# Normalising the input tiles in four pinned steps at the pace of the chunks, in a three-mixer decoder layer

## The chip, the cores and the metric

The kernel runs on one core of a Trainium2 chip. The metric is the device time of one launch in microseconds (us), the median of several runs. TensorE (PE in the profile) multiplies matrices; VectorE (DVE), ScalarE (ACT) and GpSimd (POOL) work on tiles; SyncE (SP) issues the DMAs of this kernel. Each engine works through its own list of instructions strictly in order.

## What the reference computes, cut to what matters

One layer of a decoder is applied to a prompt of 2048 tokens of 1024 features and to eight single sample tokens. All three mixers read the same normalised input h:

```python
h = rmsnorm(x, g_norm)            # x * rsqrt(mean(x*x) + EPS) * g
proj = h @ w_in_l                 # one projection, columns split among A, B, C
ya = swa_prompt(q, k, v, ...)     # A: softmax attention, window 128, 8 heads
yb, v_rows = chunk_mlp(ub, vb, ...)   # B: gated MLP in chunks of 128
oc, S_fin = gla(qc, kc, vc, ...)  # C: gated linear attention
y = concat([ya * silu(ga), yb * silu(gb), yc * silu(gc)])
x = x + y @ w_out_l               # and a last rmsnorm
```

## The kernel before, in words

**Tiles and chunks.** x comes in 16 tiles of 128 tokens (`NTILE`). Two tiles make a chunk of 256 tokens (`CT`), so there are 8 chunks. For each chunk the kernel builds `hT[c]`, the normalised input transposed to features on partitions, as two f16 parts, high and low; all eight stay in SBUF. A projection is three matmuls for each block of 128 features (`PASSES`: high*high, high*low, low*high).

**How one tile is made.** `x_load(t)` (L241) fetches 128x1024 floats into one of four buffers. `norm_split` does five things: ACT squares the tile and sums each row (L245, "square"); DVE scales the sum (L247) and takes its reciprocal root in nine instructions on one column (L125, L126, L127 and three times L131 and L135; together with L247 this is "root"); ACT writes the tile times that factor as f16 (L249, "high"); DVE computes what f16 lost (L250, "low"). `h_tile` then issues two DMA transposes on SP (L259), one for each part. `hs_prep` does the same for the eight sample tokens, and sends them through DRAM.

**Phase A, the first 310 us or so.** For each chunk PE computes two value units (evicted by ACT L471 and DVE L472), one key unit (ACT L450 and L451, DVE L452 and L453, each twice), four query units (ACT L491, DVE L492, each twice) and two gate units (ACT L501 takes the tanh, DVE L502 multiplies). The two gates of chunk c are called here its first and second gate. Chunks 0 and 1 come first with both gates behind them; from chunk 2 on the gates follow their chunk. The projection of x reads `hT[c]`, so chunk c can't begin before its tiles are transposed.

Beside it runs the softmax of 32 half-tiles, four to a chunk: scores on PE (L521), scale, bias and row maximum on DVE (L525, four to a half-tile), three small steps on DVE (L535, L537, L539), then on ACT the sink's exponent (L542), which also opens the four exponents (L553), a cast to f16 (L563), on POOL the part that f16 lost (L564), two transposes on SP (L578), and on PE the product with V (L593), evicted on DVE (L598, L600). L566, L572 and L573 on DVE are the row sums' reciprocal.

**What sets the order.** `at(t, f)` emits step f when the planned time of the matmuls emitted so far, counted from their columns, passes t. A chunk's plan is `TQ` = 15.68 for its value, key and query units and 10.24 for its two gates, so `TC` = 25.92; this clock of the plan runs faster than the chip. A scheduler then places the emitted instructions on each engine by its own estimate; only those that are wrapped in `keep_in_program_order` keep their order among one another. In the kernel before, tile t is emitted at `HT0 + HTD * (t - 4)`, 22, 33, 44 and so on, one tile for 11 planned us; that is faster than the 12.96 that half a chunk takes, and the tiles' instructions aren't pinned.

Phases B and C and the output projection follow. The weights of B (`LOADP["B0"]`, `LOADP["B1"]`) are loaded during phase A, behind the tiles.

Of the kernel before, what the change touches and what calls it, by code (L numbers as in the profile page):

```python
# [12 lines left out]
BF16 = mybir.dt.bfloat16  # L13
I32 = mybir.dt.int32
U32 = mybir.dt.uint32
AF = mybir.ActivationFunctionType
ALU = mybir.AluOpType
# [6 lines left out]
DM = 1024  # L24
DMIX = 1536
EPS = 1e-6
# [17 lines left out]
def hybrid_step_kernel(ctx: ExitStack, tc: tile.TileContext, I, O):  # L44
    nc = tc.nc
    V, S, G, PE, SP = nc.vector, nc.scalar, nc.gpsimd, nc.tensor, nc.sync
# [17 lines left out]
    HT0, HTD, HTL = 22, 11, 18  # L64
    WB = {"pha": 1, "phb": 1, "yy": 6}

    def nm(s):
        cnt[0] += 1
        return f"{s}_{cnt[0]}"
# [13 lines left out]
    def hbuf(shape, dt):  # L83
        return hp_.tile(shape, dt, tag="hT", name=nm("hb"))

    def slot(shape, dt):
        return sl_.tile(shape, dt, tag="slot", name=nm("sl"))
# [31 lines left out]
    def chain(p, n):  # L119
        t = sm.tile([p, 8 * n], F32, tag=f"ch{n}", name=nm("ch"), bufs=CHB[n])  # L120
        return [t[:, i * n:(i + 1) * n] for i in range(8)]

    def rsqrt(ch, n):
        v, vh, y, b = ch[0], ch[1], ch[2], ch[3]
        V.tensor_scalar(out=vh, in0=v, scalar1=-0.5, scalar2=None, op0=ALU.mult)  # L125
        V.tensor_scalar(out=y.bitcast(I32), in0=v.bitcast(I32), scalar1=1, scalar2=None, op0=ALU.logical_shift_right)  # L126
        V.tensor_scalar(out=y.bitcast(I32), in0=y.bitcast(I32), scalar1=-1.0, scalar2=float(0x5F3759DF),  # L127
                        op0=ALU.mult, op1=ALU.add)
        for _ in range(3):
            if n == 1:  # L130
                V.scalar_tensor_tensor(out=b, in0=y, scalar=vh, in1=y, op0=ALU.mult, op1=ALU.mult)  # L131
            else:
                V.tensor_tensor(out=b, in0=y, in1=y, op=ALU.mult)
                V.tensor_tensor(out=b, in0=b, in1=vh, op=ALU.mult)
            V.scalar_tensor_tensor(out=y, in0=b, scalar=1.5, in1=y, op0=ALU.add, op1=ALU.mult)  # L135
        return y
# [11 lines left out]
    LOADP = {}  # L148
# [67 lines left out]
    def stage_slot(n):  # L216
        def f():
            return [(slot([128, 8, n], F32), 0, 8)]
        return f

    def dst_slot(n):
        return lambda: slot([128, 2, 8, n], F16)
# [4 lines left out]
    hT = {}  # L227
    xst = {}

    def h_alloc(c):  # L230
        hT[c] = hbuf([128, 2, 8, CT], F16)

    def x_bufs(j):
        if not xst:
            xst[0], xst[1] = slot([128, 4096], F32), slot([128, 4096], F32)
        b = xst[j // 2][:, (j % 2) * 2048:(j % 2 + 1) * 2048]
        return b[:, 0:DM], b[:, DM:2 * DM].bitcast(F16).rearrange("p (a b) -> p a b", a=2)

    def x_load(t):
        xt, _ = x_bufs(t % 4)  # L240
        SP.dma_start(out=xt, in_=xp[t * 128:(t + 1) * 128, :])  # L241

    def norm_split(xt, xh, p):
        ch = chain(p, 1)
        S.activation(out=xh[:, 0, :].bitcast(BF16), in_=xt, func=AF.Square, accum_out=ch[4])  # L245
        q = 2.0 ** -20
        V.tensor_scalar(out=ch[0], in0=ch[4], scalar1=q / DM, scalar2=q * EPS, op0=ALU.mult, op1=ALU.add)  # L247
        rs = rsqrt(ch, 1)
        S.activation(out=xh[:, 0, :], in_=xt, func=AF.Copy, scale=rs)  # L249
        V.scalar_tensor_tensor(out=xh[:, 1, :], in0=xt, scalar=rs, in1=xh[:, 0, :], op0=ALU.mult, op1=ALU.subtract)  # L250

    def h_tile(t):
        c, j = divmod(t, 2)
        if j == 0:
            h_alloc(c)
        xt, xh = x_bufs(t % 4)
        norm_split(xt, xh, 128)
        for hl in range(2):
            SP.dma_start_transpose(out=hT[c][:, hl, :, j * 128:(j + 1) * 128], in_=xh[:, hl, :])  # L259

    def hs_prep():
        xt, xh = x_bufs(0)
        xt, xh = xt[:NB], xh[:NB]
        SP.dma_start(out=xt, in_=xs)
        norm_split(xt, xh, NB)
        for hl in range(2):
            SP.dma_start(out=hs_d[hl * 8:(hl + 1) * 8, :], in_=xh[:, hl, :])
        h16 = sm.tile([128, 8, 16], F16, tag="h16", name="h16", bufs=1)
        SP.dma_start_transpose(out=h16, in_=hs_d)
        G.memset(hs, 0.0)  # L270
        G.tensor_copy(out=hs[:, :, 0:16], in_=h16)
        V.tensor_reduce(out=selg, in_=ident.rearrange("p (g c) -> p c g", c=8), axis=AX.X, op=ALU.add)
# [4 lines left out]
    def at(t, *fs):  # L277
        for f in fs:
            cnt[0] += 1
            bisect.insort(EV, (t, cnt[0], f))  # L280
# [1037 lines left out]
    if True:  # L1318
# [21 lines left out]
        for f in prA0[1:]:  # L1340
# [3 lines left out]
        prB = [prep_slice(f"B{i}", 3 + i, [(OFF[n], 512)], stage_slot(512), dst_slot(512))  # L1344
               for i, n in enumerate(("vb", "gb", "ub"))]
# [16 lines left out]
        TQ, TG, TC = 15.68, 20.48, 25.92  # L1362
# [15 lines left out]
        at(7.0, lc_bm(0))  # L1378
        at(9.0, lc_bm(1))
        for t in range(4, NTILE):  # L1380
            at(HT0 + HTD * (t - 4) - HTL, lambda t=t: x_load(t))
            at(HT0 + HTD * (t - 4), lambda t=t: h_tile(t))
        at(HT0 + HTD * 12, hs_prep)
        at(11.0, prA2[1])
        at(14.0, prA2[2], prA2[3])
        at(18.0, prA2[4], consts_A)
        tb = HT0 + HTD * 12 + 4
        for f, d in zip(LOADP["B0"] + prB[0][1:], (0, 3, 6, 9, 12, 20, 21.5, 24)):
            at(tb + d, f)
        tb += 24  # L1390
        for i, f in enumerate(LOADP["B1"]):
            at(tb + 3 * i, f)
        tb = TB - 12
        for f, d in zip(prB[1][1:], (0, 8, 9.5, 11)):
            at(tb + d, f)
# [45 lines left out]
        for c in range(NCH):  # L1441
# [29 lines left out]
            if c in (4, 5, 6):  # L1471
                i = c - 4
# [71 lines left out]
```

## Time and profile before

| what | value |
|---|---|
| median of 3 runs | 1185.88 us (1183.29 to 1186.48) |
| the profiled execution: its time, its span | 1185.16 us, 1183.4 us |
| PE busy | 1127.1 us, 95% of the span, 7623 matmuls |
| DVE busy | 681.8 us, 58% |
| ACT busy | 477.1 us, 40% |
| POOL busy | 72.6 us, 6%, nearly all of it the 32 instructions of L564 |
| mean granted clock of PE | 0.988 of full speed |

The profiled execution took 1.76 us more than its span, and lies 0.7 us under the median. The busy share of PE is a mean over stages: for most of the span it has next to no idle time, and the places where it has some are in phase A.

### The profile page before, as it was taken

To read this page: it belongs to the slowest core of one execution; us is meant where nothing else is said; L and a number is where in the kernel's file an instruction comes from. 1 tells how busy PE (TensorE), PEld (TensorE's weight loads), DVE (VectorE), ACT (ScalarE), POOL (GpSimd) and SP (SyncE) were. 2 spreads that over 40 slices of the span, in tenths; PEclk is the share of its full clock that TensorE was granted. 3 is DMA by queue.
4 is the path that set the end of the run, shared out by engine and by line. 5 is a ranking of instruction groups with operands and counts; after the bars stand their busy time and mean duration, and the time that the engine had idled before them with its cause. 6 is when DMAs were issued, how large, how long until landed. Compare 5 with 4: busy or idle time off the path is not lost.

```text
span 1183.4 us, 19624 instructions
## 1 busy us (share of the span) xinstructions
PE 1127.1 (95%) x7623; PEld 661.8 (56%) x7623; DVE 681.8 (58%) x2236; ACT 477.1 (40%) x960; POOL 72.6 (6%) x49
## 2 busy tenths in 40 slices
PE   4897899997999999999999999999999999999997
PEld 3756577775645544444466567656665543444443
DVE  5896866658586355675383356744635653544442
ACT  7776665567572111553265411312312132322220
POOL 0021222222210000000000000000000000000000
PEclk9998999999899999999999999999999999999999
DMA  9579964445454012000055422220124345766641
GB/s 275 162 135 192 194 153 90 70 85 127 104 145 117 18 59 96 1 19 18 19 187 168 173 73 47 89 81 19 59 50 143 121 114 150 223 156 159 165 126 54
DMA packets 202055, 131.17 MB, mean 111 GB/s; under 512 B 160225, under 2 KB 174818, under 8 KB 201962
## 3 DMA queue, kind: packets, MB, share of 16 engines
q1 hardware_dynamic: 201962, 129.92, 42.5%
q8 instruction: 59, 0.97, 0.4%
q14 instruction: 34, 0.28, 0.1%
HBM read 67.21 MB, written 25.33 MB: 78 GB/s over the span
## 4 chain that ended last, share of the span: by engine, by line
PE 58%; DMA 5%; DVE 4%; ACT 3%; issue 1%; SPq 1%; DVEq 0%; ACTq 0%
PE pp L308 31%; PE pp L1027 13%; PE pp L297 6%; DMA hb<-sl 2%; PE mx L886 1%; PE mx L690 1%; PE mx L868 1%; ACT sl L996 1%; DMA sq_d<-yy 1%; PE mx L892 1%; PE mx L900 1%; DMA sl<-in_w_out_dram 1%; DMA sl<-y_d 1%; SPq L1008 1%; DVE sl L1016 1%
## 5 line engine op out<-in xcount | busy, mean ns | idle before, releaser
L308 PE MATMUL pp<-sl,hb 128*128 128x512 f16 x2304 | 516.3, 380 | 1.3 <-DVE qk L492 1.3
L308 PEld LDWEIGHTS <-hb 128*128 128x128 f16 x2688 | 248.4, 99 | 265.7 <-issue 8.0
L1027 PE MATMUL pp<-hb,hb 128*128 128x512 f16 x1152 | 251.1, 379 | 3.1 <-DMA hb<-sl 3.1
L1027 PEld LDWEIGHTS <-hb 128*128 128x128 f16 x1152 | 111.7, 98 | 140.9 <-DMA hb<-sl 6.2
L297 PE MATMUL pp<-hb,sl 128*128 128x256 f16 x1536 | 180.2, 276 | 10.6 <-DVE yy L502 10.5
L297 PEld LDWEIGHTS <-sl 128*128 128x128 f16 x1536 | 150.3, 99 | 34.2 <-issue 12.9
L564 POOL TENSOR_TENSOR phb<-Lp,pha 128x1024 f16<-128x1024 f32 (+1 forms) x32 | 66.5, 2077 | 283.3 <-ACT pha L563 267.1
L1030 DVE SCALAR_TENSOR_TENSOR sl<-pp,finv,sl 128x512 f32<-128x512 f32 x32 | 23.9, 747 | 86.1 <-PE pp L1027 86.0
L501 ACT ACTIVATE yy<-pp,scal 128x512 f32<-128x512 f32 x48 | 32.5, 680 | 84.9 <-PE pp L308 62.0
L1013 ACT ACTIVATE sl<-sl 128x1024 f32<-128x1024 f32 (+1 forms) x16 | 16.9, 1056 | 117.1 <-DVE sl L1030 115.0
L553 ACT ACTIVATE Lp<-Lp,sm 128x256 f32<-128x256 f32 (+1 forms) x128 | 62.3, 487 | 0.2
L525 DVE CUSTOM_DVE_ANT_0 Lp<-mx,BM,scal 128x256 f32<-128x256 f32 (+1 forms) x128 | 54.6, 471 | 2.0 <-PE mx L521 1.4
L502 DVE SCALAR_TENSOR_TENSOR yy<-yy,pp 128x512 f32<-128x512 f32 x48 | 32.7, 682 | 38.1 <-ACT yy L501 38.0
L492 DVE SCALAR_TENSOR_TENSOR qk<-pp,qk 64x256 f16<-64x256 f32 x64 | 26.9, 422 | 38.8 <-ACT qk L491 37.8
L642 ACT ACTIVATE kk<-pp,invs 128x512 f32<-128x512 f32 x16 | 10.9, 683 | 83.3 <-PE pp L308 83.3
L997 DVE SCALAR_TENSOR_TENSOR sl<-sl,ch 128x1536 f16<-128x1536 f32 (+1 forms) x17 | 30.9, 1816 | 20.4 <-ACT sl L996 20.3
L996 ACT ACTIVATE sl<-sl,ch 128x1536 f16<-128x1536 f32 (+1 forms) x17 | 26.8, 1576 | 32.1 <-DVE ch L145 32.1
L521 PE MATMUL mx<-kk,qk 128*128 128x256 f16 (+1 forms) x256 | 33.3, 271 | 3.6 <-DVE sm L525 3.6
L205 DVE SCALAR_TENSOR_TENSOR sl<-sl,gs,sl 128x512 f16<-128x512 f32 x48 | 35.1, 791 | 1.7 <-ACT sl L204 1.7
L308 PE MATMUL pp<-s,hb 128*128 128x144 f16 x384 | 29.7, 236 | 6.2 <-DMA hb<-sl 4.0
L656 DVE BATCH_NORM_STATS2 sm<-kk 128x6 f32<-128x512 f32 x16 | 11.0, 689 | 41.5 <-ACT kk L642 41.5
L563 ACT CAST pha<-Lp 128x1024 f16<-128x1024 f32 (+1 forms) x32 | 32.4, 1011 | 5.0 <-DMA pt<-pha 4.6
(316 smaller groups left out, 1227.2 us busy)
## 6 DMA issues: line engine op xcount, KB each, us to landing
sl<-in_x_prompt_dram SPq DMA_DIRECT2D x32, 512.0 KB
sl<-in_w_in_dram SPq DMA_DIRECT2D x24, 512.0 KB
sl<-in_w_out_dram SPq DMA_DIRECT2D x6, 2048.0 KB
sl<-y_d SPq DMA_DIRECT2D x16, 768.0 KB
y_d<-yy SPq DMA_DIRECT2D x32, 256.0 KB
out_dram<-sl SPq DMA_DIRECT2D x15, 512.0 KB
hb<-in_w_in_dram SPq DMA_DIRECT2D x8, 512.0 KB
y_d<-Lp SPq DMA_DIRECT2D x8, 512.0 KB
```

The source lines that it names most:

```text
L205: V.scalar_tensor_tensor(out=lo, in0=src, scalar=gk, in1=hi, op0=ALU.mult, op1=ALU.subtract)
L297: PE.matmul(ps[:m, :CT], w[:, wl, k, c0:c0 + m], h[:, hl, k, :], start=(n == 0), stop=(n == 23))
L308: PE.matmul(ps[:, :n_], h[:, hl, k, j * 128:(j + 1) * 128], w[:, wl, k, c0:c0 + n_], start=(n == 0), stop=(n == 23))
L501: S.activation(out=g, in_=ps, func=AF.Tanh, scale=hg)
L502: V.scalar_tensor_tensor(out=g, in0=g, scalar=1.0, in1=ps, op0=ALU.add, op1=ALU.mult)
L521: PE.matmul(pv[:, hh, :], Qt[c][:, h // 2, h % 2, j * 128:(j + 1) * 128], Kt[c][:, 2 * hb + hl, ko:ko + W], start=(hl == 0), stop=(hl == 1))
L525: V.tensor_tensor_reduce(out=L[:, i, :], in0=pv[:, hh, :], in1=BM["t"][:, 4 * hb + i, 256 - W:256], scale=cS, scalar=-3e38, op0=ALU.add, o ...
L553: S.activation(out=L[:, i, :], in_=L[:, i, :], func=AF.Exp, bias=nb[:, i:i + 1], accum_out=den[:, i:i + 1])
L563: S.copy(P[0], L)
L564: G.tensor_tensor(out=P[1], in0=L, in1=P[0], op=ALU.subtract)
L996: S.activation(out=d["h"][:, 0, :], in_=d["y"], func=AF.Copy, scale=s)
L1027: PE.matmul(ps, d["yT"][:, hl, k, :], wo[k // 2][:, wl, k % 2, cs], start=(n == 0), stop=(n == 35))
```

## The change

`norm_split` and `h_tile` stay for the first four tiles and the samples. For tiles 4 to 15 a new `h_steps(t)` returns the same work as four functions, and the loop emits them at four planned times: square at `th`, root 5 later, high 9 later, low with both transposes 11 later. `th` follows the chunk: 22, 29.84, 43.76, 55.76, 69.7, 81.7, 95.6, 107.6, 121.5, 133.5, 147.4 and 159.4 for tiles 4 to 15, so two tiles for each 25.92 planned us. The first instruction of each step is pinned. `x_load` stays 18 ahead of its tile. The samples' preparation moves from 154 to 173.4, the loads and preparation of B0 from 158 to 167.4 with shorter distances, B1's loads from 182 to 180.4 and closer together.

```diff
+    def h_steps(t):
+        st = {}
+        def square():
+            if t % 2 == 0:
+                h_alloc(t // 2)
+            st["x"], st["h"] = x_bufs(t % 4)
+            st["ch"] = chain(128, 1)
+            tc.keep_in_program_order(S.activation(out=st["h"][:, 0, :].bitcast(BF16), in_=st["x"], func=AF.Square,
+                                                  accum_out=st["ch"][4]))
+        def root():
+            ch = st["ch"]
+            q = 2.0 ** -20
+            tc.keep_in_program_order(V.tensor_scalar(out=ch[0], in0=ch[4], scalar1=q / DM, scalar2=q * EPS,
+                                                     op0=ALU.mult, op1=ALU.add))
+            st["rs"] = rsqrt(ch, 1)
+        def high():
+            tc.keep_in_program_order(S.activation(out=st["h"][:, 0, :], in_=st["x"], func=AF.Copy, scale=st["rs"]))
+        def low():
+            tc.keep_in_program_order(V.scalar_tensor_tensor(out=st["h"][:, 1, :], in0=st["x"], scalar=st["rs"],
+                                                            in1=st["h"][:, 0, :], op0=ALU.mult, op1=ALU.subtract))
+            c, j = divmod(t, 2)
+            for hl in range(2):
+                SP.dma_start_transpose(out=hT[c][:, hl, :, j * 128:(j + 1) * 128], in_=st["h"][:, hl, :])
+        return square, root, high, low
...
-            at(HT0 + HTD * (t - 4) - HTL, lambda t=t: x_load(t))
-            at(HT0 + HTD * (t - 4), lambda t=t: h_tile(t))
-        at(HT0 + HTD * 12, hs_prep)
+            th = max(HT0, 2 * TQ + TG + TC * (t // 2 - 2) - 34 + 12 * (t % 2))
+            at(th - HTL, lambda t=t: x_load(t))
+            for f, d in zip(h_steps(t), (0, 5, 9, 11)):
+                at(th + d, f)
+        at(th + 14, hs_prep)
...
-        tb = HT0 + HTD * 12 + 4
-        for f, d in zip(LOADP["B0"] + prB[0][1:], (0, 3, 6, 9, 12, 20, 21.5, 24)):
+        tb = th + 8
+        for f, d in zip(LOADP["B0"] + prB[0][1:], (0, 2, 4, 6, 10, 18, 19.5, 21)):
...
-        tb += 24
+        tb += 13
         for i, f in enumerate(LOADP["B1"]):
-            at(tb + 3 * i, f)
+            at(tb + 2 * i, f)
```

In the changed kernel the new function pushes every later line 30 down: L502 becomes L532, L525 becomes L555, L566 becomes L596, L472 becomes L502, and so on. Its four steps are L260 (square), L266 (root, with L125 to L135), L271 (high) and L274 (low).

Three places show what the change does to an order. The first is DVE at the second gate of chunk 1 in the kernel before, where the low steps (L250) of three tiles stand among softmax and key evictions:

```order
L566 TENSOR_TENSOR sm_1357<-sm_1235,sm_1236 128x4
L250 SCALAR_TENSOR_TENSOR sl_107<-sl_107,ch_2052 128x1024
L572 RECIPROCAL sm_1359<-sm_1357 128x4
L535 TENSOR_TENSOR sm_1416<-sm_1326,sinkb 128x4
L598 TENSOR_TENSOR yy_1216<-mx_1379,rc_980 128x256
L573 TENSOR_SCALAR rc_1181<-sm_1359,scal 128x4
L452 SCALAR_TENSOR_TENSOR kk_1365<-pp_1296,kk_1365 64x256
L453 SCALAR_TENSOR_TENSOR kk_1365<-pp_1296,kk_1365 64x256
L600 TENSOR_TENSOR yy_1216<-yy_1216,yy_1034 128x256
L537 TENSOR_SCALAR sm_1418<-sm_1416 128x4
L250 SCALAR_TENSOR_TENSOR sl_107<-sl_107,ch_2300 128x1024
```

By the end of chunk 2's second gate all sixteen tiles have been made in the kernel before; from chunk 3 on DVE's order holds no tile. The second place is DVE at the first gate of chunk 4 in the changed kernel, where the root of an even tile (here tile 12) now stands between the gate and the four scores of the next half-tile (L555); in the kernel before L525 follows L502 here without anything between:

```order
L532 SCALAR_TENSOR_TENSOR yy_2857<-yy_2857,pp_2760 128x512
L266 TENSOR_SCALAR ch_2792<-ch_2792 128x1
L125 TENSOR_SCALAR ch_2792<-ch_2792 128x1
L126 TENSOR_SCALAR ch_2792<-ch_2792 128x1
L127 TENSOR_SCALAR ch_2792<-ch_2792 128x1
L131 SCALAR_TENSOR_TENSOR ch_2792<-ch_2792 128x1
L135 SCALAR_TENSOR_TENSOR ch_2792<-ch_2792 128x1
L131 SCALAR_TENSOR_TENSOR ch_2792<-ch_2792 128x1
L135 SCALAR_TENSOR_TENSOR ch_2792<-ch_2792 128x1
L131 SCALAR_TENSOR_TENSOR ch_2792<-ch_2792 128x1
L135 SCALAR_TENSOR_TENSOR ch_2792<-ch_2792 128x1
L555 ISA Lp_2888,sm_2889<-mx_2890,BM,scal 128x256
```

The same ten instructions stand there in chunks 2 to 5. The third place is DVE a little later, behind the second gate of chunk 4: the low step of tile 12 (L274) now stands between the second value eviction and the next four scores.

```order
L532 SCALAR_TENSOR_TENSOR yy_2955<-yy_2955,pp_2860 128x512
L502 SCALAR_TENSOR_TENSOR vt_2995<-pp_2958,vt_2995 128x2x64
L504 TENSOR_SCALAR LR<-pp_2958,invs 128x16
L502 SCALAR_TENSOR_TENSOR vt_3024<-pp_2999,vt_3024 128x2x64
L504 TENSOR_SCALAR LR<-pp_2999,invs 128x16
L274 SCALAR_TENSOR_TENSOR sl_106<-sl_106,ch_2792 128x1024
L555 ISA Lp_3051,sm_3052<-mx_3053,BM,scal 128x256
L555 ISA sm_3052 128x1
```

The odd tile of the chunk follows in the same way: its root stands among the query evictions, its low step behind the scores and small steps of the third half-tile. On ACT the high step of the even tile stands behind the second gate, before the value evictions, and the square of the odd tile behind these. So chunks 2 to 6 each have two tiles between their predecessor's gates and their own.

## Rows read from the trace of the kernel before

**Rows 1.** The page, chain of work that ended last, shares by engine.

```profile
PE 58%; DMA 5%; DVE 4%; ACT 3%; issue 1%; SPq 1%; DVEq 0%; ACTq 0%
```

**Rows 2.** Windows: stretch, its length, busy us (instructions), PE's granted clock, DMA share.

```profile
91.44:140.03 48.59, 37.52 (x345) 27.29 (x344) 35.08 (x153) 33.40 (x79) 8.51 (x4) 0.86 1.02 195
...
209.00:241.76 32.76, 32.76 (x351) 25.36 (x348) 21.73 (x90) 18.69 (x56) 9.60 (x5) 1.00 0.48 82
...
276.71:311.50 34.79, 28.92 (x290) 23.01 (x287) 25.52 (x88) 20.35 (x54) 7.89 (x6) 0.85 0.53 140
```

**Rows 3.** Waits of PE, 91 to 345 us: total, times, longest.

```profile
PE pp L297 <- DVE yy L502: 10.5, 3, 7.9
PE mx L458 <- DVE sm L456: 5.0, 1, 5.0
```

**Rows 4.** Timeline of SP and ACT before the longest stall.

```profile
82.02 9.45 SPq L259 DMA_TRANSPOSE hb<-sl  x6
98.63 1.04 ACT L563 CAST pha<-Lp 128x1024 f16<-128x1024 f32 x1 [4.57 <-DMA pt<-pha]
```

**Rows 5.** Timeline of DVE: gate evictions (start, length).

```profile
92.07 0.69 DVE L502 SCALAR_TENSOR_TENSOR yy<-yy,pp 128x512 f32<-128x512 f32 x1 [1.05 <-ACT yy L501]
105.31 0.69 DVE L502 SCALAR_TENSOR_TENSOR yy<-yy,pp 128x512 f32<-128x512 f32 x1 [0.44 <-ACT yy L501]
139.38 0.68 DVE L502 SCALAR_TENSOR_TENSOR yy<-yy,pp 128x512 f32<-128x512 f32 x1
147.34 0.67 DVE L502 SCALAR_TENSOR_TENSOR yy<-yy,pp 128x512 f32<-128x512 f32 x1
176.31 0.69 DVE L502 SCALAR_TENSOR_TENSOR yy<-yy,pp 128x512 f32<-128x512 f32 x1 [2.16 <-ACT yy L501]
207.62 0.69 DVE L502 SCALAR_TENSOR_TENSOR yy<-yy,pp 128x512 f32<-128x512 f32 x1 [2.15 <-ACT yy L501]
239.31 0.69 DVE L502 SCALAR_TENSOR_TENSOR yy<-yy,pp 128x512 f32<-128x512 f32 x1 [2.16 <-ACT yy L501]
275.20 0.69 DVE L502 SCALAR_TENSOR_TENSOR yy<-yy,pp 128x512 f32<-128x512 f32 x1 [2.02 <-ACT yy L501]
```

**Rows 6.** Waits of ACT, 91 to 277 us: total, times, longest.

```profile
ACT sm L542 <- DVE sm L539: 40.5, 16, 3.5
```

**Rows 7.** Groups of DVE instructions, 105.3 to 147.4 us.

```profile
L250 DVE SCALAR_TENSOR_TENSOR sl<-sl,ch 128x1024 f16<-128x1024 f32 (+1 forms) x7 | 8.9, 1278 | 0.8 <-ACT sl L249 0.8
```

**Rows 8.** Timeline of POOL, DVE and ACT behind the first gate of chunk 4.

```profile
208.60 2.13 POOL L564 TENSOR_TENSOR phb<-Lp,pha 128x1024 f16<-128x1024 f32 x1 [5.99 <-ACT pha L563]
...
209.84 0.91 DVE L566 TENSOR_TENSOR sm<-sm,sm 128x4 f32<-128x4 f32 x1
...
211.53 0.20 ACT L542 ACTIVATE sm<-sm 128x4 f32<-128x4 f32 x1 [3.01 <-DVE sm L539]
```

**Rows 9.** Timeline of DVE: one root, begun at 84.65 and ended after 90.86.

```profile
84.65 0.14 DVE L247 TENSOR_SCALAR ch<-ch 128x1 f32<-128x1 f32 x1
...
85.26 0.22 DVE L131 SCALAR_TENSOR_TENSOR ch<-ch 128x1 f32<-128x1 f32 x1
...
90.41 0.16 DVE L135 SCALAR_TENSOR_TENSOR ch<-ch 128x1 f32<-128x1 f32 x1
...
90.86 0.16 DVE L135 SCALAR_TENSOR_TENSOR ch<-ch 128x1 f32<-128x1 f32 x1
```

**Rows 10.** Timeline of POOL and DVE at 61 us.

```profile
61.36 1.16 POOL L564 TENSOR_TENSOR phb<-Lp,pha 128x512 f16<-128x512 f32 x1 [59.29 <-ACT pha L563]
...
61.69 0.83 DVE L135 SCALAR_TENSOR_TENSOR ch<-ch 128x1 f32<-128x1 f32 x1
```

**Rows 11.** Timeline of ACT, one high step; of DVE and POOL, the value evictions of chunk 5.

```profile
92.93 1.14 ACT L249 ACTIVATE sl<-sl,ch 128x1024 f16<-128x1024 f32 x1
...
215.60 0.29 DVE L472 SCALAR_TENSOR_TENSOR vt<-pp,vt 128x128 f16<-128x128 f32 x1 [0.70 <-ACT vt L471]
...
215.47 2.13 POOL L564 TENSOR_TENSOR phb<-Lp,pha 128x1024 f16<-128x1024 f32 x1 [4.74 <-ACT pha L563]
```

## The prediction

> **What bounds the kernel.** The chain of waits first: PE holds 58% of it [rows 1], a mean that hides the stages. So next the windows by chunk [rows 2]. From 209 to 241.76 us PE is busy for all of its 32.76 us: that is PE's own pace for a chunk of phase A. From 91.44 to 140.03 it is busy for 37.52 of 48.59 us at a granted clock of 0.86, and from 276.71 to 311.5 for 28.92 of 34.79 at 0.85. PE's waits say for whom [rows 3]: 10.5 us for gate evictions on DVE (once 7.9) and 5.0 for one small DVE step, L456. Behind about 345 us PE has hardly a gap, and the change leaves the order there nearly as it was, so I take what phase A gains or loses to reach the end one to one.
>
> The timeline shows what makes the 7.9. Six tile transposes in a row occupy SP from 82.02 for 9.45 us; the transposes of the softmax stand behind them; ACT's cast L563 waits 4.57 us for these [rows 4]; the gate that stands behind on ACT, and with it DVE's L502 at 105.31, comes late [rows 5].
>
> Then the pace of DVE and ACT, read from the first gates of the chunks [rows 5]: 92.07, 139.38, 176.31, 207.62, 239.31, 275.20, so 47.31, 36.93, 31.31, 31.69 and 35.89 us apart. (275.20 stands behind B0's first preparation and the sample's steps.) In the two periods without a tile (31.31 and 31.69) this pair needs only 1.1 to 1.5 us less than PE. DVE is busy for just 21.73 of 32.76 us there [rows 2], but the rest is no free room: DVE and ACT wait for each other, ACT 40.5 us in 16 waits for L539 alone [rows 6]. What stands in series in that loop lengthens it.
>
> So the kernel before makes its tiles early, at a high price in chunks 1 and 2, and runs chunks 3 to 5 near PE's pace. The changed one spreads them: two in each of five periods.
>
> **The change, part by part.** It removes nothing: each tile costs one root and one low step on DVE, one square and one high step on ACT, two transposes on SP. What counts is where they stand. Two prices for a tile bound the answer.
>
> Packed: from the second gate of chunk 1 to that of chunk 2, 105.31 to 147.34, the loop took 42.03 us [rows 5], with seven low steps in it [rows 7]; two of their roots began earlier, so I count six and a half tiles. (42.03 - 31.5) / 6.5 = 1.6 us for a tile, filled into gaps between other work. Two to a period would give 31.5 + 3.2 = 34.7 us.
>
> In series: I walk the new order from the first gate of chunk 4 at T0 = 207.62.
> - Root, even tile. One root takes 0.61 us from L247 to the first L131 [rows 9], then three pairs of L131 and L135 at 0.45 (90.41 to 90.86): 1.96. Now it stands between the gate and the four scores. There POOL's L564 runs from 208.60 to 210.73 [rows 8]. In the rows a DVE instruction with two SBUF inputs doesn't end while L564 runs: L135, a column of 128, took 0.83 us at 61.69 and ended at 62.52, as POOL did (61.36 + 1.16) [rows 10]; L566 took 0.91 at 209.84 and ended at 210.75 [rows 8]. L131 reads a tile twice and would come at T0 + 1.21, inside L564. I take it as held to T0 + 3.11; the root ends at 4.1, the four scores, 1.62 long (L566 follows them at T0 + 2.22, and they start 0.6 behind the gate), at 5.74, and some 0.9 later (0.78 from the end of L566 to the exponents, and L566 itself, unheld) ACT can start its exponents, at 6.67 where it was 3.91 (211.53). That is 2.76 late. Without the hold: root at 2.56, scores at 4.2, L566 no longer held, exponents at 5.1: 1.2 late.
> - High, even tile, 1.14 [rows 11]: stands on ACT ahead of the value evictions, for which DVE waits: 1.05 late, less the little that they wait anyway.
> - Low, even tile: 1.27 [rows 7], between the last value eviction and four scores. POOL starts L564 just ahead of that eviction (215.47 and 215.60) [rows 11]. The rows show no low step that begins inside an L564. Bounds: 1.27 alone, or 1.27 and up to 2.13 more. It reads two SBUF tiles as L566 does, so I take it as held for what is left of L564 then, 1.45: 2.7 late.
> - The small step that releases the next exponents now stands behind the second pair of key evictions, in the kernel before ahead of it: 1.1 late, an estimate (two DVE evictions and ACT's turn between them).
> - Root, odd tile: 1.96 in pieces between query evictions, L131 inside an L564 for up to 2.0 more; part of that lies beside ACT's query evictions. 3.3 with the hold, 1.7 without, of 4.0 and 1.96.
> - High and low of the odd tile and the squares: beside waits that these delays make. At nothing; if that cover fails, 1.1 and 1.3 more.
>
> With holds 2.76 + 1.05 + 2.7 + 1.1 + 3.3 = 10.9, of which I let 0.9 be taken up by waits later in the loop: a period of 41.5. Without holds 1.2 + 1.05 + 1.27 + 1.1 + 1.7 = 6.3, less 0.9: 36.9. I take the holds, since both rows that look at such a pair show them.
>
> The Trainium skill, page "SBUF — State Buffer", section "Who interferes with whom", has VectorE instructions with two SBUF inputs share a port pair with GpSimd, and whoever comes first blocks the other for a whole instruction. The rows on L135 and L566 agree; none shows the low step, which by that rule is held too. By a reading in which only the low step escapes, each of five periods would be 1.45 us shorter and the sum 7 us lower.
>
> **The sum**, against the profiled execution's own 1185.16 (0.7 us under the median of the runs shown):
> - first gates of chunk 1 to 2: 47.3 becomes 41.5, -5.8 (the 9.45 us of transposes on SP is split up, so its stall goes; the new loop remains)
> - chunk 2 to 3: 36.9 becomes 41.5, +4.6
> - chunk 3 to 4: 31.3 becomes 41.5, +10.2
> - chunk 4 to 5: 31.7 becomes 41.5, +9.8
> - chunk 5 to 6: 35.9 becomes 44, +8.1 (41.5, and 2.5 of the 4.2 that B0 and the samples add there now)
> - chunk 1's first gate itself comes earlier, three tiles fewer before it: -2, bounds 0 and 3 x 1.6 = -4.8
> - chunk 7: its 5.0 us wait and slow clock shrink when PE comes later than DVE: -3, bounds 0 and -7.
>
> Together +21.9: 1207. With a period P in place of 41.5 the sum is 5P - 185.6, so it turns from a loss to a gain below P = 37.1.
>
> PE then waits some 9 us in each chunk for a gate's bank. The granted clock was 0.86 in the stretch with the 7.9 us stall [rows 2]; more such stretches would slow matmuls, but there PE isn't what is waited for, so I add nothing.
>
> DMA: the tiles' transposes stand on SP ahead of some softmax transposes. Single pairs instead of six at once take 2 x 1.6 us (9.45 / 6 each) and fit into SP's gaps. The samples' last transpose now waits behind three loads of B0; its readers on PE run late enough. At nothing; if they had to wait, a stall like the 5.0 us of L456 [rows 3] is the upper bound.
>
> **Rivals.**
> 1. Faster: the steps fall into the waits of the loop, as in the packed stretch: a period of 34.7. Then -12.6 - 2.2 + 3.4 + 3.0 + 3 (with all of the 4.2) - 2 - 4 = -11.4: 1174. For it: DVE and ACT have 10 us and more of waits in a period, and 1.6 us for a tile has been measured on this loop, with holds in it. Against: there the scheduler had put low steps and roots where others waited, and DVE was full; in the new order roots and the even low step stand ahead of scores, on which ACT waits. It decides below a period of 37.
> 2. Same: in series but without holds, a period of 36.9. Then -10.4 + 0 + 5.6 + 5.2 + 3.5 - 2 - 3 = -1.1: 1184. For it: holds move as L564 moves, and the new steps shift both. Against: the root comes 0.6 us behind the gate and L564 follows the gate by 1 us, both set by ACT's order.
> 3. The pace doesn't matter, because PE's gaps were made by other things: SP's transposes stay bunched and the 7.9 us stall returns. Then the first term is nearer 0 and the time 1210 or above. Against: in the new SP order no more than two tile transposes follow each other ahead of a softmax pair.
>
> **How the numbers follow.** In series with holds 0.56, with a range of its own of 1195 to 1218 (period 39 to 44); the packed loop 0.30; without holds 0.12; the third 0.02, as slow as the first. A measurement of this kernel tells 0.3%, 3.6 us, from no change. The middle case is spread over both sides of it and the same (0.03, 0.06, 0.03); of the packed one 0.01 falls within it; so faster 0.32, same 0.07, slower 0.61. I put the time at that of the likeliest, 1207. The range goes from 1172, in the packed case, to 1217.
>
> **What would show it.** First gates of chunks 2 to 6 some 41 us apart (packed: 33 to 35); the first L131 behind the gate of chunks 2 to 5 at about 2 us instead of 0.22, ending with L564; low steps behind the value evictions at 2.7 instead of 1.27; ACT's waits for the last small step longer, PE's waits for gate evictions some 40 us instead of 10.5; no row of six tile transposes on SP. It is wrong if the first gates follow at PE's 32.76, above all if ACT doesn't wait longer for the small steps, for then the tiles lay in gaps.

## The result and the profile after

The changed kernel takes 1219.18 us (median of 5 runs, 1217.88 to 1223.63) against 1185.12 us of the kernel before beside it: a ratio of 1.0295, 95% interval 1.0277 to 1.0312. It is slower by 34 us. The sign was forecast; the forecast was 22 us and its range ended at 1217.

The windows of the changed kernel, from the first gate of each chunk to that of the next (length, busy us of PE, PEld, DVE, ACT, POOL, clock, DMA share, GB/s), answer to [rows 2]:

```profile
89.36:130.53 41.17, 36.72 (x371) 28.02 (x370) 29.81 (x106) 23.75 (x65) 8.51 (x4) 0.96 0.61 118
130.53:172.74 42.21, 36.05 (x364) 27.49 (x362) 30.91 (x105) 23.03 (x63) 8.50 (x4) 0.96 0.56 108
172.74:215.91 43.17, 34.34 (x329) 24.45 (x327) 30.56 (x105) 22.65 (x61) 8.50 (x4) 0.96 0.56 115
215.91:258.01 42.10, 34.99 (x349) 26.48 (x347) 29.58 (x106) 23.63 (x65) 9.01 (x4) 0.96 0.53 90
258.01:306.70 48.69, 35.17 (x315) 25.53 (x313) 34.59 (x125) 28.55 (x72) 9.29 (x5) 0.82 0.56 116
```

Four periods of 41.2 to 43.2 us, where [rows 5] have 47.3, 36.9, 31.3 and 31.7, and a fifth of 48.7 against 35.9. DVE is still busy for only some 30 of 42 us, and PE has idle time in every period, 40.1 us in the five together. PE's waits, 60 to 400 us, answer to [rows 3]:

```profile
PE mx L551 <- DVE sm L555: 17.8, 10, 2.9
PE pp L327 <- DVE yy L532: 12.8, 5, 2.9
PE mx L351 <- POOL hs L301: 9.6, 1, 9.6
PE mx L488 <- DVE sm L486: 4.3, 1, 4.3
```

Scores and gate evictions of DVE make 30.6 us of waits, in 15 pieces, none as long as the one of 7.9 before. One wait is new: PE stood for 9.6 us until POOL had copied the transposed samples (L301).

ACT's waits for DVE grew as well. Between the first gates of chunks 1 and 6 the kernel before (91 to 277 us) has these beside the 40.5 us of [rows 6]:

```profile
ACT kk L450 <- DVE kk L453: 10.1, 5, 2.8
ACT qk L491 <- DVE qk L492: 3.5, 7, 0.5
```

and the changed kernel (91 to 300 us) has, in the same stretch of the program:

```profile
ACT sm L572 <- DVE sm L569: 51.7, 19, 5.8
ACT kk L480 <- DVE kk L483: 16.8, 5, 4.0
ACT sl L271 <- DVE ch L135: 10.6, 5, 3.0
ACT qk L521 <- DVE qk L522: 10.3, 7, 2.5
```

So 89.4 us where it was 54.1, 35.3 more; that stretch itself became 34.2 us longer (217.3 against 183.1).

The timeline behind the first gate of chunk 4 shows the root as it was walked in the prediction:

```profile
215.91 0.69 DVE L532 SCALAR_TENSOR_TENSOR yy<-yy,pp 128x512 f32<-128x512 f32 x1 [2.07 <-ACT yy L531]
216.52 0.15 DVE L266 TENSOR_SCALAR ch<-ch 128x1 f32<-128x1 f32 x1
...
217.58 2.12 DVE L131 SCALAR_TENSOR_TENSOR ch<-ch 128x1 f32<-128x1 f32 x1
...
217.56 2.12 POOL L594 TENSOR_TENSOR phb<-Lp,pha 128x1024 f16<-128x1024 f32 x1 [5.07 <-ACT pha L593]
...
222.87 0.20 ACT L572 ACTIVATE sm<-sm 128x4 f32<-128x4 f32 x1 [5.38 <-DVE sm L569]
```

L131 works on one column and took 0.22 us wherever nothing stood against it; here it took 2.12 and ended with POOL's subtraction (217.56 + 2.12 = 219.68, L131 at 219.70). ACT's exponents came 6.96 us behind the gate, where the prediction said 6.67 and the kernel before had 3.91.

The groups of DVE from 89.3 to 258 us, four periods, show what such holds add up to:

```profile
L131 DVE SCALAR_TENSOR_TENSOR ch<-ch 128x1 f32<-128x1 f32 x24 | 18.7, 780 | 0.8
L274 DVE SCALAR_TENSOR_TENSOR sl<-sl,ch 128x1024 f16<-128x1024 f32 x8 | 14.6, 1824 | 0.1
L596 DVE TENSOR_TENSOR sm<-sm,sm 128x4 f32<-128x4 f32 x16 | 4.1, 254 | 0.0
```

24 times 0.22 would be 5.3, so L131 was held for 13.4 us; 8 times 1.28 would be 10.2, so the low steps were held for 4.4. Two of the even ones, the first begun inside an L594, the second ahead of one:

```profile
101.95 2.72 DVE L274 SCALAR_TENSOR_TENSOR sl<-sl,ch 128x1024 f16<-128x1024 f32 x1
...
228.39 1.28 DVE L274 SCALAR_TENSOR_TENSOR sl<-sl,ch 128x1024 f16<-128x1024 f32 x1
...
229.02 2.63 POOL L594 TENSOR_TENSOR phb<-Lp,pha 128x1024 f16<-128x1024 f32 x1 [9.34 <-ACT pha L593]
```

The new wait on the samples is read in three timelines of the changed kernel (SP, POOL, PE):

```profile
291.42 1.23 SPq L278 DMA_TRANSPOSE hb<-sl  x1
292.83 1.48 SPq L165 DMA_DIRECT2D sl<-in_w_in_dram  x3
294.36 1.14 SPq L299 DMA_TRANSPOSE h<-hs_d  x1
...
300.61 0.29 POOL L301 COPY hs<-h 128x128 f16<-128x128 f16 x1 [4.70 <-DMA h<-hs_d]
...
300.95 1.10 PE L351 MATMUL mx<-s,hs 128*32 128x272 f16 x16 [9.62 <-POOL hs L301]
```

The samples' transpose (L299) stands on SP behind the last tile's transpose and three loads of B0, was issued at 294.36, and POOL's copy of it could start only 6.2 us later; PE's own order had reached L351 at 291.3 (300.95 less the 9.62 of waiting).

### The profile page after: what moved, and what is told of

Its sections match the earlier page's. It is cut to its first block, busy times and chain, and to the rows that moved or that the text cites. A ratio compares the mean times of both kernels' runs of the same rounds, so it can differ in the third digit from the quotient of the medians.

```text
span 1217.3 us, 19627 instructions
## 1 busy us (share of the span) xinstructions
PE 1136.4 (93%) x7623; PEld 665.5 (55%) x7623; DVE 710.0 (58%) x2236; ACT 478.2 (39%) x960; POOL 73.4 (6%) x49
## 3 DMA queue, kind: packets, MB, share of 16 engines
q1 hardware_dynamic: 201962, 129.92, 41.4%
## 4 chain that ended last, share of the span: by engine, by line
PE 57%; DMA 4%; DVE 3%; ACT 2%; issue 1%; SPq 1%; DVEq 0%; ACTq 0%
PE pp L338 31%; PE pp L1057 14%; PE pp L327 6%; DMA hb<-sl 2%; PE mx L916 1%; PE mx L720 1%; PE mx L898 1%; DMA sq_d<-yy 1%; PE mx L922 1%; PE mx L930 1%; DMA sl<-in_w_out_dram 1%; DMA sl<-y_d 1%; ACT sl L1026 1%; PE mx L351 1%; DVE sl L1046 1%
## 5 line engine op out<-in xcount | busy, mean ns | idle before, releaser
L338 PEld LDWEIGHTS <-hb 128*128 128x128 f16 x2688 | 249.0, 99 | 266.5 <-issue 10.2
L327 PE MATMUL pp<-hb,sl 128*128 128x256 f16 x1536 | 182.2, 278 | 13.0 <-DVE yy L532 12.8
L594 POOL TENSOR_TENSOR phb<-Lp,pha 128x1024 f16<-128x1024 f32 (+1 forms) x32 | 67.3, 2103 | 299.8 <-ACT pha L593 266.1
L532 DVE SCALAR_TENSOR_TENSOR yy<-yy,pp 128x512 f32<-128x512 f32 x48 | 32.8, 683 | 43.1 <-ACT yy L531 43.0
L555 DVE CUSTOM_DVE_ANT_0 Lp<-mx,BM,scal 128x256 f32<-128x256 f32 (+1 forms) x128 | 54.6, 475 | 1.1 <-PE mx L551 0.7
L551 PE MATMUL mx<-kk,qk 128*128 128x256 f16 (+1 forms) x256 | 35.2, 271 | 18.9 <-DVE sm L555 17.8
L131 DVE SCALAR_TENSOR_TENSOR ch<-ch 128x1 f32<-128x1 f32 (+2 forms) x108 | 40.5, 375 | 3.3
L551 PEld LDWEIGHTS <-qk 128*128 128x128 f16 x256 | 24.4, 98 | 28.2 <-issue 19.7
L205 DVE SCALAR_TENSOR_TENSOR sl<-sl,gs,sl 128x512 f16<-128x512 f32 x48 | 36.6, 822 | 2.3 <-ACT sl L204 2.2
```

The lines of the kernel that those rows point to most:

```text
L205: V.scalar_tensor_tensor(out=lo, in0=src, scalar=gk, in1=hi, op0=ALU.mult, op1=ALU.subtract)
L327: PE.matmul(ps[:m, :CT], w[:, wl, k, c0:c0 + m], h[:, hl, k, :], start=(n == 0), stop=(n == 23))
L338: PE.matmul(ps[:, :n_], h[:, hl, k, j * 128:(j + 1) * 128], w[:, wl, k, c0:c0 + n_], start=(n == 0), stop=(n == 23))
L532: V.scalar_tensor_tensor(out=g, in0=g, scalar=1.0, in1=ps, op0=ALU.add, op1=ALU.mult)
L551: PE.matmul(pv[:, hh, :], Qt[c][:, h // 2, h % 2, j * 128:(j + 1) * 128], Kt[c][:, 2 * hb + hl, ko:ko + W], start=(hl == 0), stop=(hl == 1))
L555: V.tensor_tensor_reduce(out=L[:, i, :], in0=pv[:, hh, :], in1=BM["t"][:, 4 * hb + i, 256 - W:256], scale=cS, scalar=-3e38, op0=ALU.add, o ...
```

## The experiments

The theory: the pinned steps stand in series in the loop of DVE and ACT, and POOL's subtraction holds those that read two SBUF tiles (a hold: a DVE instruction takes longer, up to the end of a POOL instruction); with a wait on the samples behind it. Its rivals: the later planned times cost in themselves (PE waits for input tiles); the pins cost wherever the steps stand; the holds are small beside the series.

**Samples earlier (hs_early).**

```diff
-        at(th + 14, hs_prep)
+        at(140.0, hs_prep)
```

> The changed kernel with only the samples' preparation emitted earlier (planned 140 instead of 173.4). If PE's 9.6 us wait for the samples' transposed copy is a cost of its own beside the loop, it goes and the time falls by 7 to 10 us, to 1209 to 1212. If the wait only stands where PE would have waited for DVE and ACT anyway (the loop is the bound there too), the time stays at 1217 to 1220 and the wait turns up as waits for gate evictions and scores.

Measured: 1213.13 us, ratio 1.0233 (1.0212 to 1.0254), so 6 us less than the changed kernel, a little short of the 7 to 10 expected. The 9.6 us wait is gone; in its place PE waits 3.5 us at the same matmul, now for DVE:

```profile
PE mx L351 <- DVE sm L555: 3.5, 1, 3.5
```

The first gates of chunks 5 and 6 are 41.4 us apart here (259.06 and 300.47) instead of 48.7. Chunk 6 to 7 gives some of that back: 47.3 instead of 45.7.

**The same times without pins (no_pin).** In `h_steps` the four calls stay, without `keep_in_program_order` around them.

> The changed kernel with the four steps at the same planned times, but not pinned; the scheduler then places them early again. If the lengthened loop is what costs (steps pinned in series), the periods of chunks 3 to 5 return to 31 to 33 us and the time to 1178 to 1192. If the later planned times cost in themselves, periods of about 40 us and 1205 to 1220.

Measured: 1185.99 us, ratio 1.0006 (0.9995 to 1.0017), no change against the kernel before. The periods of chunks 3 to 5 are what they were, and PE has no idle time in the second:

```profile
174.93:206.24 31.31, 30.79 (x308) 23.63 (x306) 20.80 (x83) 18.46 (x57) 8.51 (x4) 1.00 0.47 85
206.24:237.93 31.69, 31.69 (x340) 24.88 (x339) 20.67 (x84) 18.69 (x57) 8.53 (x4) 1.00 0.49 85
```

The planned times alone decide nothing here: the scheduler places unpinned steps early again. The last tile's low step starts at 140.30 us, in the kernel before at 141.92, in the changed one at 290.10.

**The pace without steps (pace_tiles).** The kernel before with the new formula for `th` in the loop of `x_load` and `h_tile`.

> The kernel before with only the planned times of its loads and whole tiles at the pace of the chunks; nothing split or pinned, the samples and B0 as before. If pins are what spreads the tiles, this order stays close to that of before and the time is 1181 to 1190, no change. If the pace is what costs, 1205 to 1220.

Measured: 1185.49 us, ratio 1.0002 (0.9989 to 1.0014). No change. But the last tile's low step starts at 145.14 us here: the planned pace didn't spread the unpinned tiles. So this run says nothing of what spread tiles cost; that is left to `moved` below, which keeps pins and pace.

**POOL reads nothing (after_no_read, before_no_read).**

```diff
-            G.tensor_tensor(out=P[1], in0=L, in1=P[0], op=ALU.subtract)
+            G.memset(P[1], 0.0)
```

> The changed kernel with POOL's subtraction of each half-tile replaced by a fill with zeros: it leaves out the low part of the softmax weights, so POOL reads nothing from SBUF. If holds by POOL's reads make up the series (some 2 us at each root), roots take 2 us instead of 3.9, periods fall from 42 to about 38 and the time by 13 to 20 us, to 1199 to 1206. If the series alone costs, periods of 41 to 42 and 1214 to 1220.

> The kernel before with POOL's subtraction replaced by a fill with zeros (leaves out the low part of the softmax weights), the control for the same edit on the changed kernel, which gained 37 us there. If that gain came from holds of the new steps, this one gains only what L566 and B0's preparation lose to POOL: 1172 to 1182. If it came from the softmax running without its low part (earlier fills, fewer waits), this one falls as far too: 1145 to 1160.

Measured: 1181.83 us for the changed kernel, ratio 0.9970 (0.9960 to 0.9981), which is 37 us less than with the subtraction; 1178.99 for the kernel before, ratio 0.9942 (0.9923 to 0.9962), 7 us less. I had expected 13 to 20 us of the first. The control speaks for holds as the cause, since the same edit gives only 7 in the kernel before. But not all of the difference of 30 us belongs to the tiles' steps: in the profiled executions (35.7 us apart) 24.3 us are gained ahead of the first gate of chunk 6, where the steps stand, and 11.4 behind it, where there is none (table below). In the changed kernel without reads no hold is left on the steps; the windows and groups of DVE (88.5 to 237.3 us) read:

```profile
88.56:125.00 36.44, 36.44 (x395) 27.96 (x394) 25.90 (x105) 23.19 (x64) 4.11 (x5) 1.00 0.77 149
125.00:162.35 37.35, 35.01 (x355) 26.86 (x353) 25.54 (x105) 23.61 (x64) 3.76 (x5) 0.95 0.64 128
162.35:199.55 37.20, 34.53 (x344) 26.08 (x342) 25.23 (x105) 22.67 (x61) 3.55 (x4) 0.95 0.64 129
199.55:237.36 37.81, 33.52 (x353) 25.64 (x351) 25.35 (x105) 23.64 (x65) 4.76 (x5) 1.00 0.55 100
```

```profile
L274 DVE SCALAR_TENSOR_TENSOR sl<-sl,ch 128x1024 f16<-128x1024 f32 x8 | 10.2, 1280 | 0.1
L131 DVE SCALAR_TENSOR_TENSOR ch<-ch 128x1 f32<-128x1 f32 x24 | 5.3, 219 | 0.8
```

From the first gate of chunk 1 to that of chunk 6 DVE's order is the same, instruction by instruction; the periods are some 37 us instead of 42 (the gate that ends the first lies at 125.57). This edit also lets the fills start before ACT's cast, so it takes away a little more than the reads; the next experiment doesn't.

**POOL's subtraction in four pieces (after_split4, before_split4).**

```diff
-            G.tensor_tensor(out=P[1], in0=L, in1=P[0], op=ALU.subtract)
+            for i in range(4):
+                G.tensor_tensor(out=P[1][:, i, :], in0=L[:, i, :], in1=P[0][:, i, :], op=ALU.subtract)
```

> The changed kernel with POOL's subtraction in four instructions of 256 columns instead of one of 1024; the same work, the same order on DVE. If DVE is held to the end of one POOL instruction, holds shrink from some 2 us to 0.7 at most, periods from 42 to 38 or 39, and the time to 1198 to 1207. If DVE is held as long as POOL has work, nothing changes or it gets worse by POOL's longer total: 1217 to 1225.

> The kernel before with the same split of POOL's subtraction. L566 was held for up to 0.9 to 1.3 us several times in a chunk and L205 for 2: if holds end with one POOL instruction, 1176 to 1184; if POOL's longer total delays the softmax's second transposes more than that, 1185 to 1192.

Measured: 1200.99 us for the changed kernel, ratio 1.0130 (1.0112 to 1.0148), 18 us less for the same work in the same order of DVE. Of the 19.9 us between the two profiled executions 10.8 lie ahead of the first gate of chunk 6 and 9.1 behind it. For the kernel before 1185.80, ratio 0.9998 (0.9989 to 1.0007): nothing, where 1176 to 1184 was expected if holds end with one POOL instruction. (No single L205 in the trace of the kernel before took the 2 us of that expectation; the longest took 1.11.) POOL and DVE behind the first gate of chunk 3, changed kernel with the split:

```profile
167.81 2.55 POOL L595 TENSOR_TENSOR phb<-Lp,pha 128x256 f16<-128x256 f32 x4 [4.22 <-ACT pha L593]
...
168.06 0.44 DVE L131 SCALAR_TENSOR_TENSOR ch<-ch 128x1 f32<-128x1 f32 x1
...
168.53 0.59 DVE L135 SCALAR_TENSOR_TENSOR ch<-ch 128x1 f32<-128x1 f32 x1
169.16 0.59 DVE L131 SCALAR_TENSOR_TENSOR ch<-ch 128x1 f32<-128x1 f32 x1
169.79 0.59 DVE L135 SCALAR_TENSOR_TENSOR ch<-ch 128x1 f32<-128x1 f32 x1
```

DVE gets in between the pieces, and is held again by the next one: one small instruction for each piece. So a hold ends with one POOL instruction, not with POOL's work. Its periods are 38.3, 40.3, 40.3 and 41.0, between the two others and longer than the 38 or 39 expected; the time came out as expected because of the 9.1 us behind them.

**The root behind the exponents' release (root_8), and with the samples earlier (root_8_hs).**

```diff
-            for f, d in zip(h_steps(t), (0, 5, 9, 11)):
+            for f, d in zip(h_steps(t), (0, 8, 9, 11)):
```

> The changed kernel with one number changed: the root step is emitted 8 behind the square instead of 5, so the even root stands behind the small step that releases the exponents, outside POOL's subtraction, and the odd one behind the scores of its half-tile. The walk prices the root's place at 2.8 (even) and up to 3.3 (odd) in each of five periods: periods of 37 to 39 us and 1192 to 1202, with the samples' wait of some 9 us still in it. If the root's place were not what costs, 1214 to 1222.

> The changed kernel with the root 8 behind the square, and the samples' preparation at 150 as in the moved kernel; low and high steps stay at 11 and 9. PE's 9.0 us wait for the samples' copy goes. If it stands in series with the loop, 1192 to 1196, and what is left to the moved kernel's 1187 is the low and high steps' place. If the loop fills it, 1198 to 1203.

Measured: 1201.34 us, ratio 1.0123 (1.0107 to 1.0138), for one number changed: 18 us less than with 5. The root then stands behind the scores as well as outside POOL's subtraction, so this run prices the place as a whole. No L131 is longer than 0.221 us, and first gates are 37.4, 38.1, 38.3 and 38.4 us apart. L596 now meets POOL instead; over four periods (92.2 to 244.3 us) it takes 12.9 us where it took 4.1:

```profile
L596 DVE TENSOR_TENSOR sm<-sm,sm 128x4 f32<-128x4 f32 x16 | 12.9, 807 | 0.0
L274 DVE SCALAR_TENSOR_TENSOR sl<-sl,ch 128x1024 f16<-128x1024 f32 x8 | 11.9, 1490 | 5.0 <-ACT sl L271 5.0
```

With the samples' preparation at 150 too: 1196.29, ratio 1.0078 (1.0056 to 1.0099), another 5 us, 0.3 past the 1192 to 1196 expected. As in the first experiment the 9.0 us wait for POOL's copy becomes a wait of 4.9 us for DVE at the same matmul.

**All four steps moved (moved), and earlier (earlier, earlier_split4).** `moved` has steps at (0, 8, 10, 15) and the samples at 150: root and low step stand behind the release of a half-tile's exponents. `earlier` takes each tile half a chunk sooner:

```diff
+            th = max(HT0 - 2 + t % 2, 2 * TQ + TG + TC * (t // 2 - 2) - 34 - 13.92 * (1 - t % 2))
```

> The changed kernel with the same pace and pins, but the steps at 0, 8, 10 and 15 instead of 0, 5, 9 and 11, which puts the even root behind the small step that releases ACT's exponents and the low steps behind those of their half-tile; the samples' preparation at 150. If what costs is steps in series ahead of the scores, inside POOL's subtraction, periods fall to 33 to 35 and the time to 1178 to 1192. If pins or the pace cost wherever the steps stand, 1205 to 1215.

> The steps at the places of the moved kernel, with each tile half a chunk earlier, so that a chunk's transposes are there before PE asks. The 7.8 us that PE waited there for the transposes go: 1178 to 1184, a little faster than the kernel before. If the tiles then lengthen the first chunks as much as they did in the kernel before, 1184 to 1190.

> The same with POOL's subtraction in four instructions. With roots and low steps mostly outside POOL's work the split has little left to shorten: 1175 to 1184. If POOL's longer total delays the softmax's transposes, 1184 to 1190.

Measured: `moved` 1187.47 us, ratio 1.0019 (1.0010 to 1.0029); periods of 33.9, 35.7, 34.7 and 35.5, pinned and at the pace of the chunks as before. So neither pins nor pace cost 34 us; the places of the steps do, with 5 to 6 us for the samples, which this run moves too. PE's largest sum of waits in it was for the tiles' transposes, which come late for their chunk:

```profile
PE pp L338 <- DMA hb<-sl: 7.8, 4, 3.1
PE mx L351 <- DVE sm L555: 5.1, 1, 5.1
```

`earlier` takes these 7.8 us away but gains nothing, 1187.42, ratio 1.0015 (1.0006 to 1.0023), not the 1178 to 1184 expected: PE's waits for gate evictions grew from 1.0 to 7.9 us. `earlier_split4` 1184.03, ratio 0.9979 (0.9968 to 0.9990): the only version with all of the work that is measurably ahead of the kernel before, by 0.2%, which is within the 0.3% that I called no change.

Where each run gained or lost its time, read from one profiled execution each (us; whole executions of one kernel differ by some 5, so differences of a few us say little):

| run | start to the first gate of chunk 6 | from there to the end |
|---|---|---|
| before | 275.2 | 908.2 |
| before_no_read | 272.3 | 907.4 |
| before_split4 | 272.9 | 907.9 |
| after | 306.7 | 910.6 |
| hs_early | 300.5 | 912.5 |
| root_8 | 288.1 | 913.5 |
| root_8_hs | 282.8 | 912.5 |
| moved | 271.3 | 914.1 |
| earlier | 274.7 | 910.6 |
| earlier_split4 | 275.2 | 905.0 |
| after_split4 | 295.9 | 901.5 |
| after_no_read | 282.4 | 899.2 |

With the steps in better places (`moved`) the stretch with the tiles is 3.9 us shorter than in the kernel before, and what lies behind it, where no tile is made, 5.9 longer. Both are at the edge of what one execution of each can tell; the 9 to 11 us that after_split4 and after_no_read gain behind the tiles are clear of it.

## Why the prediction was right in kind and wrong in size

Term by term, in the first gates of both kernels:

| term | forecast | measured |
|---|---|---|
| first gate of chunk 1 | -2 | -2.7 |
| chunk 1 to 2 | -5.8 | -6.1 |
| chunk 2 to 3 | +4.6 | +5.3 |
| chunk 3 to 4 | +10.2 | +11.9 |
| chunk 4 to 5 | +9.8 | +10.4 |
| chunk 5 to 6 | +8.1 | +12.8 |
| chunk 6 to 7 and the rest | -3 | +2.4 |
| sum | +21.9 | +33.9 |

- **What bounds it**: right. DVE and ACT pace phase A in the changed kernel (ACT's waits for DVE grew by 35.3 us, the stretch by 34.2), and the loss of phase A reaches the end: from the first gate of chunk 7 on the two spans differ by 1.3 us only.
- **The period in series with holds**: 41.5 forecast, 41.2 to 43.2 measured. Without holds 36.9 forecast, 36.8 to 37.8 measured in the kernel without reads, whose fills also start earlier. The sums fit; of their parts only the root and the even low step were measured by themselves, so that the rest fits as well isn't shown. One part put at nothing shows in the trace: the odd tile's high step waits for its root on ACT, 1.5 to 3.0 us in each of five periods (L271 for L135). The packed price of 1.6 us was nearest to the moved kernel (34.7 forecast, 33.9 to 35.7 measured). One of the seven low steps it was counted from is the samples' (8x1024, 1.26 us at 146.14), about as long as a tile's.
- **The root**: the hold measured 2.12, the exponents 6.96 us behind the gate (6.67 forecast). A small miss in it: of the five even roots behind a first gate, three had the first L131 caught (1.89 us) and two, this one among them, the second.
- **PE's waits**: some 40 us for gate evictions were forecast. PE's idle time came to 40.1 us, but only 12.8 of it for gate evictions; 17.8 were for scores and 9.6 for the samples.
- **The low step**: the rows of before showed none inside an L564; the changed kernel shows three of four even low steps in four periods at 2.7 us, 1.45 more than alone, which is what I had put. At 228.39 the low step began 0.63 ahead of L594 (229.02), ran in 1.28, and L594 took 2.63 instead of 2.13: whoever came first held the other. The Trainium skill, page "SBUF — State Buffer", section "Who interferes with whom", says that the order of issue decides who blocks; these rows agree.
- **What failed, first term**: "The samples' last transpose now waits behind three loads of B0; its readers on PE run late enough. At nothing". They didn't. PE reached the samples' matmul 9.6 us ahead of the copy, and the upper bound I gave, 5.0, was too low as well. Taking that wait away gives 6 us in the changed kernel (5 in root_8_hs), since 3.5 to 4.9 us of another wait in the same place stay. It is more than the 4.7 us by which chunk 5 to 6 came out longer than forecast: with the samples earlier that period took 41.4 us, 2.6 below the 44 forecast.
- **What failed, second term**: "chunk 7: its 5.0 us wait and slow clock shrink". The wait stayed (4.3 us at L488), and PE's granted clock was 0.82 from 258 to 306.7 us and still 0.91 from 306 to 345 (0.85 in [rows 2] for the same stage). I had a gain of 3 there and got a loss of 2.4. The walk priced holds on the tiles' steps only; the trace shows one on B0's preparation, which the change had moved. The step that makes B0's scales, L193, took 0.23 us at 276.81 in the kernel before. In the changed one it begins inside an L594 and ends with the two fills that follow on POOL (317.45 + 0.98 = 318.43; L193 at 318.46):

```profile
315.39 2.12 POOL L594 TENSOR_TENSOR phb<-Lp,pha 128x1024 f16<-128x1024 f32 x1 [3.54 <-DVE ch L140]
317.45 0.98 POOL L827 MEMSET s1c<- 128x512 f32 x2
...
315.79 2.67 DVE L193 TENSOR_SCALAR gs<-gcol,ch 128x8 f32<-128x8 f32 x1
...
324.65 0.45 PE L488 MATMUL mx<-ident,sm 128*128 128x128 f32 x1 [4.31 <-DVE sm L486]
```

ACT's split of B0 (L204) waits 4.35 us for it, the key evictions stand behind that on ACT, and PE's L488 waits for these by way of DVE's L486. With the subtraction in four pieces L193 took 0.30 us, without reads 0.23; there PE waited 1.5 and 1.3 us at L488, its granted clock was 1.00 from chunk 6's first gate to chunk 7's (0.93 in the changed kernel), and that stretch took 38.3 and 37.3 us instead of 45.7 (44.6 in the kernel before). In `moved` L193 took 1.61 us, PE waited 4.0 at L488, and the stretch took 49.7. So a gain was to be had there, and it is missing in every run in which L193 was held. L193 isn't the whole of it: in `earlier` it took 0.23 us, and the stretch took 45.6 all the same, with a wait of 4.6 at L488. That is read from the traces; no run moved L193 alone, so how much of the 5.4 us that this term missed is the hold, and how much the clock, stays open.
- **The range**: with 44 for chunk 5 to 6 and a gain in chunk 7 as the likeliest values, 1217 as the end left only 10 us for both to go wrong; they took 10, and the four periods with chunk 1's first gate 2 more.

Where the 34 us went, by experiment: root's place 18 (root_8); the samples 5 to 6 (root_8_hs against root_8, hs_early); low and high steps' place another 9 (moved against root_8_hs); the rest, some 2 us, is what `moved` still lacks to the kernel before. These steps share holds, and other orders of taking them away would divide the sum otherwise. Taking POOL's reads away (after_no_read) brings back 24.3 of the 31.5 us by which the changed kernel comes later to chunk 6's first gate; in the kernel before the same edit brings 2.9 there.

## What to carry to other kernels

When two engines wait on each other in a loop, their idle time is not room: ask of every instruction put into it whether it stands ahead of the step that releases the other engine. A pin fixes where a step stands, so a pin made by a plan's clock is only as good as the plan's idea of where the gaps are; one number moved by three planned microseconds was worth 18 us. And moving a chain later, look for its last reader and for the queue that its last DMA stands in: that reader may be the one engine with nothing to spare. When a test edit gives the time that you expected, look in which stage it gave it: nearly half of what the split subtraction gained lay where none of the steps under test stands.

## What was not expected of the hardware

- A DVE instruction on a single column (128x1, both inputs in SBUF) is held by a POOL instruction for up to its whole length: 0.22 us became 1.33 to 2.17. With POOL's work in four pieces (0.73 us each in the mean, from the groups of POOL's instructions) small DVE instructions came through one for each piece, 0.44 to 0.59 us apiece in the rows shown, and the low steps, held to 2.73 before, took 1.28. With POOL only writing (a fill), all 24 of them took 0.22.
- A DVE instruction with one tile and a column of factors as inputs took longer beside POOL too: L193 (128x8) took 2.67 us instead of 0.23 and ended with a subtraction and two fills on POOL.
- Removing a hold can hand it on: with the root out of the way, L596 took it over, from 4.1 to 12.9 us in four periods, and the time still fell by 18.
- A wait of PE taken away was worth 5 to 6 of 9 us, since PE then waited 3.5 to 4.9 us for DVE at the same matmul.
